# Unit 1 weighed in two pairs, and the prior laid out on 64 partitions

## The chip, the cores and the metric

The kernel runs on one core of a Trainium2 chip. The metric is the device time of one execution in microseconds (us); a number of executions are timed and their median is given. Beside the timed ones there is one profiled execution, whose records make up the profile and the trace.

## The reference

For each of 4096 rows (32 x 128) there are four heads of 4096 logits and four prior values. Each head's logits go through a softmax, the prior's four values go through a softmax, and the result is the mixture of the four heads by the prior.

```python
batch, seq, vocab = 32, 128, 4096
num_heads = 4
...
prior_probs = np.exp(prior - prior.max(axis=-1, keepdims=True))
prior_probs = prior_probs / prior_probs.sum(axis=-1, keepdims=True)
softmax = np.exp(logits - logits.max(axis=-1, keepdims=True))
softmax = softmax / softmax.sum(axis=-1, keepdims=True)
mixture = np.sum(prior_probs[..., None] * softmax, axis=2)
```

All is float32: 268 MB of logits are read, 67 MB of output are written, and the prior is 64 KB. The kernel takes the exp of the logits without subtracting their maximum.

## The kernel before

The 4096 rows are 32 units of 128 rows, one row on each partition. A unit has 8 MB of logits (four heads of 128 x 4096) and 2 MB of output. One Python loop over the units writes out the instructions; the order on each engine is the order written, apart from a few moves made at the end. Waits are given by hand: `only(ins, *keep)` leaves an instruction nothing to wait for but what it is given and what stands before it on its engine.

**Loads.** `load(u)` (line 111) issues the logits of unit u on ACT's DMA queue into `ltile[:, u % 2]`, so there are two slots. Units 0 and 28 to 30 are loaded in two halves, unit 31 in three parts, all others in one transfer of 8 MB. Loads 0 and 1 are issued at the start and wait for nothing. Load u of the later units waits for the first product of unit u - 2, which is the last to read that slot:

```python
if u >= 2:
    only(ld, adds[u - 2, 0] if h == 0 else exps[u - 2, to - 1])
```

While `late` holds, load u + 1 is written in the loop of unit u and then moved by `ahead` to stand on ACT just before the first exp of unit u. It is ACT that issues it, so what stands behind it on ACT comes after it, and it comes after what stands before.

**Exps.** For each head, ACT takes the exp of 128 x 4096 logits and sums the rows into `dsum` (line 176). Head 0 is done in place in `ltile`, heads 1 to 3 go to `ebuf1`, `ebuf2` (in PSUM) and `ebuf3`. The exp of head 1 waits for the second sum of the unit before, that of head 2 for its last sum, and in the middle units that of head 3 waits for the store of unit u - 2 (`free`).

**Weighing.** `weigh(h, n)` takes the reciprocal of n row sums on DVE (line 185), behind the last of their exps, and multiplies by the prior's n columns on GpSimd (POOL, line 187), which gives `coeff`. `sets` says which heads are weighed at once: all four in units 0 to 27, in pairs and single ones in the last four.

**Product and sums.** DVE multiplies head 0 by its coefficient into `obuf` (line 194, `adds[u, 0]`) and then adds heads 1 to 3 one after the other (line 200, `adds[u, 1]` to `adds[u, 3]`).

**Stores.** Unit u - 1 is stored (line 124) from SP's DMA queue, behind its last sum. The last units are stored from ACT's queue.

**Prior.** At the start SP issues the prior's load (line 149), 32 partitions of 128 rows with four values each. `early_transfers` moves it, and ACT's first load, ahead of the opening barrier. DVE subtracts the maximum (lines 151 and 152), ACT takes the exp (line 153, on ACT behind the three loads and ahead of the exps of unit 0), DVE sums, takes the reciprocal and multiplies (lines 154 to 156) and transposes 32 x 32 blocks into `pp` in four instructions (line 162). `pp[p, j, h, 2 g + 1]` is then the prior of row p, unit 2 g + j, head h. The first to read it is the coefficient of unit 0.

Of the kernel before, what the change touches and what calls it, by code (L numbers as in the profile page):

```python
# [7 lines left out]
FP32 = mybir.dt.float32  # L8
# [39 lines left out]
def kernel(  # L48
# [6 lines left out]
    nc = tc.nc  # L55
# [3 lines left out]
    B, S, H, V = logits.shape  # L59
    assert prior.shape == (B, S, H)  # L60
    assert out.shape == (B, S, V)
    P = 128
    J = 2
    R = P * J
    G = B * S // R
    U = G * J
# [1 line left out]

    lg = logits.rearrange("b s h v -> (b s) h v").rearrange("(g p j) h v -> g j p h v", p=P, j=J)
    ov = out.rearrange("b s v -> (b s) v").rearrange("(g p j) v -> g j p v", p=P, j=J)  # L70
    pv = prior.rearrange("b s h -> (b s) h").rearrange("(k r) h -> k r h", r=P)

    cpool = ctx.enter_context(tc.tile_pool(name="cpool", bufs=1))
    psum = ctx.enter_context(tc.tile_pool(name="psum", bufs=1, space=bass.MemoryType.PSUM))
# [5 lines left out]
    def only(ins, *keep):  # L80
        for k in keep:
            tc.add_manual_dep(
                ins.ins,
                k.ins.name,
                mybir.DependencyInfo(mybir.DependencyClass.Sync, mybir.DependencyReason.DATA),
                reason="all that this instruction waits for",
            )
        tc.declare_no_dep(
            ins.ins,
            group="loop",  # L90
            keep=[k.ins for k in keep] + before.get(ins.ins.engine, []),
            reason="covered by the waits that are kept",
        )
        tc.add_to_no_dep_group("loop", ins.ins)
        before[ins.ins.engine] = [ins.ins]
        return ins
# [2 lines left out]
    ltile = cpool.tile([P, 2, H, V], FP32, name="ltile")  # L99
    loads = {}  # L100
    exps = {}
    adds = {}
    stores = {}

    def load(u):
        if u == 0 or u >= U - 3:
            cuts = (0, 2, 3, 4) if u == U - 1 else (0, 2, 4)
        else:
            cuts = (0, H)
        for h, to in zip(cuts, cuts[1:]):  # L110
            ld = nc.scalar.dma_start(  # L111
                out=ltile[:, u % 2, h:to], in_=lg[u // J, u % J, :, h:to, :]
            )


            if u >= 2:
                only(ld, adds[u - 2, 0] if h == 0 else exps[u - 2, to - 1])
            else:
                only(ld)
            for k in range(h, to):  # L120
                loads[u, k] = ld

    def store(u, acc, eng, lo=0, hi=V):
        st = eng.dma_start(out=ov[u // J, u % J, :, lo:hi], in_=acc[:, lo:hi])
        stores[u] = only(st, adds[u, H - 1])

    assert 2 * G == 32
    pr = cpool.tile([2 * G, P, H], FP32, name="pr")  # L130
    pn = cpool.tile([2 * G, H, P], FP32, name="pn")
    pmax = cpool.tile([2 * G, P], FP32, name="pmax")
    pp = cpool.tile([P, J, H, 2 * G + 1], FP32, name="pp")


    dsum = cpool.tile([P, U, H], FP32, name="dsum")
# [9 lines left out]

    with tc.manual_schedule():
        load(0)
        nc.sync.dma_start(out=pr, in_=pv)
        load(1)  # L150
        nc.vector.reduce_max(pmax, pr, axis=AX.X)  # L151
        nc.vector.tensor_sub(pr, pr, pmax.unsqueeze(2).to_broadcast([2 * G, P, H]))  # L152
        nc.scalar.activation(pr, pr, AF.Exp)  # L153
        nc.vector.reduce_sum(pmax, pr, axis=AX.X)  # L154
        nc.vector.reciprocal(pmax, pmax)  # L155
        nc.vector.tensor_mul(  # L156
            pn.rearrange("k h r -> k r h"), pr, pmax.unsqueeze(2).to_broadcast([2 * G, P, H])
        )
        pq = pn.rearrange("k h (p j) -> k j h p", j=J)
        for t in range(P // 32):  # L160
            c = 1 - t // 2
            nc.vector.transpose(  # L162
                pp[32 * t : 32 * (t + 1), :, :, c : c + 2 * G],
                pq[:, :, :, 32 * (t % 2) : 32 * (t % 2 + 1)],
            )

        late = False
        for u in range(U):
            bufd = u < U - 2
            lt = ltile[:, u % 2]  # L170
            acc = obuf[:, u % 2] if bufd else lt[:, 0]
            es = (lt[:, 0], ebuf1, ebuf2, ebuf3) if bufd else [lt[:, h] for h in range(H)]
            ppu = pp[:, u % J, :, 2 * (u // J) + 1]

            def exp(h, *keep):
                ex = nc.scalar.activation(  # L176
                    es[h], lt[:, h], AF.Exp, accum_out=dsum[:, u, h : h + 1]
                )
                keep = (loads[u, h],) + keep
                if bufd and u and h in (1, 2):  # L180
                    keep += (adds[u - 1, 1 if h == 1 else H - 1],)
                exps[u, h] = only(ex, *keep)

            def weigh(h, n, *keep):
                rc = nc.vector.reciprocal(rden[:, u, h : h + n], dsum[:, u, h : h + n])  # L185
                only(rc, exps[u, h + n - 1])
                mul = nc.gpsimd.tensor_mul(  # L187
                    coeff[:, u, h : h + n], rden[:, u, h : h + n], ppu[:, h : h + n]
                )
                return only(mul, rc, *keep)  # L190

            def add(h, mul, lo=0, hi=V):
                if h == 0:
                    st = nc.vector.tensor_scalar(  # L194
                        out=acc[:, lo:hi], in0=es[h][:, lo:hi], scalar1=coeff[:, u, h : h + 1],
                        scalar2=None, op0=ALU.mult,
                    )
                    adds[u, h] = only(st, mul)
                else:
                    st = nc.vector.scalar_tensor_tensor(  # L200
                        out=acc[:, lo:hi], in0=es[h][:, lo:hi], scalar=coeff[:, u, h : h + 1],
                        in1=acc[:, lo:hi], op0=ALU.mult, op1=ALU.add,
                    )
                    adds[u, h] = only(st, mul, adds[u, h - 1])

            free = (stores[u - 2],) if bufd and u >= 2 else ()

            if u < U - 4:  # L210
                sets = ((0, H),)
            elif u == U - 2:
                sets = ((0, 2), (2, 3), (3, 4))
            else:
                sets = ((0, 2), (2, 4))
            for h in range(H):
                if h == 2 and 0 < u < U - 3:
                    store(u - 1, obuf[:, (u - 1) % 2], nc.sync)
                if h == 2 and u == U - 1:
                    store(u - 1, ltile[:, (u - 1) % 2, 0], nc.scalar)  # L220
                if h == 1 and late:
                    load(u + 1)
                    pairs.append((loads[u + 1, 0].ins, exps[u, 0].ins))
                    late = False
                exp(h, *(free if sets[0][1] == H and h == H - 1 else ()))
                g = next((g for g, to in sets if to == h + 1), None)
                if g is None:
                    continue
                mul = weigh(g, h + 1 - g, *(free if g == 0 and h < H - 1 else ()))
                for k in range(g, h + 1):  # L230
                    n = 2 if u == U - 1 and k == H - 1 else 1
                    w = V // n
                    for c in range(n):
                        add(k, mul, c * w, (c + 1) * w)
                        if n > 1:
                            store(u, acc, nc.scalar, c * w, (c + 1) * w)


            late = u + 2 < U - 3
            if u + 2 < U and not late:  # L240
                load(u + 2)

            if u == U - 2:
                for k in (u - 2, u - 1):
                    store(k, obuf[:, k % 2], nc.scalar)
# [30 lines left out]
```

The softmax here doesn't subtract the row's maximum and nothing guards it: scores larger than these inputs give would overflow.

## Time and profile before

| | us |
|---|---|
| median of 3 timed executions | 780.8 (780.71 to 780.85) |
| the profiled execution | 780.91 |
| its span, first to last record | 779.1 |
| exp of 128 x 4096 on ACT, mean | 3.60 |
| product on DVE (line 194), mean | 2.35 |
| one sum on DVE (line 200), mean | 4.48 |
| reciprocal 128x4, 128x2, 128x1 on DVE, mean | 0.178, 0.163, 0.157 |
| coefficient 128x4, 128x2 on POOL, mean | 0.203, 0.197 |
| issue to landing of an 8 MB load, median | 29.6 |
| issue to landing of the prior's 64 KB | 2.5 |

Times inside the profile are counted from the start of the span. A line of the timeline gives start, length, engine, source line, operation, output and input with shapes, how many instructions are merged, and in brackets the idle time of the engine just before and what ended it. "ACTq" and "SPq" are DMA issues on ACT and SP: their length is that of issuing, not of the transfer. A DMA share of 1.00 means that all 16 DMA engines of the core are moving data; in stretches of a few us the share can exceed 1, as a packet is put down to the stretch in which it is recorded.

### The profile page before, as it was taken

Reading aid. Unit: us, or ns where it says so; the run is one execution under the profiler, and the core shown is the slowest. Engines: PE = TensorE matmul, PEld = TensorE weight load, DVE = VectorE, ACT = ScalarE, POOL = GpSimd, SP = SyncE. Lnnn points to the kernel's source line nnn. Section 1 sums busy time; section 2 is a strip of 40 time slices with the busy share of each in tenths; the row PEclk is TensorE's granted clock in tenths of the full one; section 3 lists DMA queues with packets and bytes.
Section 4 is the critical chain, followed back from the end, with each engine's and each line's share of the span. In section 5 each row is a group of like instructions: output and inputs, shape, how many; then the busy total and the mean of one; then the engine's idle time right before and its main releaser. Section 6 shows DMA issues by size and latency. Waiting matters only on the chain.

```text
span 779.1 us, 620 instructions
## 1 busy us (share of the span) xinstructions
DVE 517.7 (66%) x175; ACT 472.2 (61%) x258; POOL 7.6 (1%) x41
## 2 busy tenths in 40 slices
DVE  2447865568655686556875558755577555788986
ACT  4376555765557755577555675556755567557782
POOL 0000000000000000000000000000000000000000
DMA  9999999999999999999999999999999999999998
GB/s 407 458 417 400 475 404 431 431 465 424 404 468 401 463 417 423 452 448 414 417 468 407 458 404 468 421 413 448 416 459 417 457 405 464 410 429 431 432 428 379
DMA packets 10131, 335.64 MB, mean 431 GB/s; under 512 B 1136, under 2 KB 1136, under 8 KB 1168
## 3 DMA queue, kind: packets, MB, share of 16 engines
q10 hardware_dynamic: 6048, 276.83, 82.2%
q1 hardware_dynamic: 4080, 58.79, 17.6%
q14 instruction: 3, 0.02, 0.0%
HBM read 268.50 MB, written 67.11 MB: 431 GB/s over the span
## 4 chain that ended last, share of the span: by engine, by line
DMA 60%; DVE 28%; ACT 9%; issue 2%; POOL 0%; DVEq 0%; ACTq 0%; POOLq 0%
DMA out_dram<-obuf 47%; DVE obuf L200 23%; DMA ltile<-in_logits_dram 13%; ACT ebuf L176 8%; DVE obuf L194 4%; DVE ltile L200 1%; ACT ltile L176 1%; POOL coeff L187 0%; DVE rden L185 0%; DVEq L271 0%; ACTq L111 0%; POOLq L271 0%; ACTq L176 0%
## 5 line engine op out<-in xcount | busy, mean ns | idle before, releaser
L200 DVE SCALAR_TENSOR_TENSOR obuf<-ebuf,coeff,obuf 128x4096 f32<-128x4096 f32 x90 | 403.6, 4484 | 3.8 <-POOL coeff L187 0.6
L176 ACT ACTIVATE ebuf<-ltile 128x4096 f32<-128x4096 f32 x90 | 324.1, 3601 | 33.3 <-DVE obuf L200 19.4
L176 ACT ACTIVATE ltile<-ltile 128x4096 f32<-128x4096 f32 x38 | 137.4, 3615 | 255.4 <-DMA ltile<-in_logits_dram 255.0
L185 DVE RECIPROCAL rden<-dsum 128x4 f32<-128x4 f32 (+2 forms) x37 | 6.4, 174 | 235.9 <-ACT ebuf L176 233.2
L194 DVE TENSOR_SCALAR obuf<-ltile,coeff 128x4096 f32<-128x4096 f32 x30 | 70.6, 2353 | 10.9 <-POOL coeff L187 10.9
L200 DVE SCALAR_TENSOR_TENSOR ltile<-ltile,coeff 128x4096 f32<-128x4096 f32 (+1 forms) x7 | 27.0, 3874 | 1.0 <-POOL coeff L187 0.9
L176 ACT ACTIVATION_READ_ACCUMULATOR ebuf<-ltile 128x1 f32 x90 | 16.8, 187 | 0.0
L187 POOL TENSOR_TENSOR coeff<-rden,pp 128x4 f32<-128x4 f32 (+2 forms) x37 | 7.4, 201 | 756.2 <-DVE rden L185 745.6
L176 ACT ACTIVATION_READ_ACCUMULATOR ltile<-ltile 128x1 f32 x38 | 7.1, 186 | 0.0
L194 DVE TENSOR_SCALAR ltile<-ltile,coeff 128x4096 f32<-128x4096 f32 x2 | 4.7, 2353 | 0.6 <-POOL coeff L187 0.6
L153 ACT ACT_TABLE_LOAD x1 | 1.3, 1283 | 2.2 <-issue 2.2
L151 DVE TENSOR_REDUCE pmax<-pr 32x128 f32<-32x512 f32 x1 | 0.7, 674 | 2.5 <-DMA pr<-in_prior_dram 2.5
L162 DVE STREAM_TRANSPOSE pp<-pn 32x256 f32<-32x256 f32 x4 | 1.7, 435 | 0.1
L154 DVE TENSOR_REDUCE pmax<-pr 32x128 f32<-32x512 f32 x1 | 0.7, 674 | 0.7 <-ACT pr L153 0.7
L156 DVE TENSOR_TENSOR pn<-pr,pmax 32x512 f32<-32x512 f32 x1 | 1.0, 1019 | 0.0
L155 DVE RECIPROCAL pmax<-pmax 32x128 f32<-32x128 f32 x1 | 0.9, 941 | 0.0
L153 ACT ACTIVATE pr<-pr 32x512 f32<-32x512 f32 x1 | 0.6, 628 | 0.5 <-DVE pr L152 0.5
L152 DVE TENSOR_TENSOR pr<-pr,pmax 32x512 f32<-32x512 f32 x1 | 0.7, 679 | 0.0
L260 POOL MEMSET const-bfloat16-1.0<- 128x1 bf16 x1 | 0.1, 102 | 0.0
L260 POOL MEMSET const-uint8-127<- 128x1 uint8 x1 | 0.1, 102 | 0.0
L260 POOL MEMSET const-float32-0.0<- 128x1 f32 x1 | 0.1, 99 | 0.2 <-issue 0.2
L260 POOL MEMSET const-float32-1.0<- 128x1 f32 x1 | 0.1, 99 | 0.0
## 6 DMA issues: line engine op xcount, KB each, us to landing
out_dram<-obuf SPq DMA_DIRECT2D x28, 2048.0 KB, 28.1
ltile<-in_logits_dram ACTq DMA_DIRECT2D x7, 4096.0 KB, 25.5
ltile<-in_logits_dram ACTq DMA_DIRECT2D x2, 2048.0 KB, 30.9
out_dram<-obuf ACTq DMA_DIRECT2D x2, 2048.0 KB, 26.6
out_dram<-ltile ACTq DMA_DIRECT2D x1, 2048.0 KB, 19.3
out_dram<-ltile ACTq DMA_DIRECT2D x2, 1024.0 KB, 4.8
ltile<-in_logits_dram ACTq DMA_DIRECT2D x28, 29.6
pr<-in_prior_dram SPq DMA_DIRECT2D x1, 64.0 KB, 2.5
```

Of the source, the lines that this page charges most:

```text
L151: nc.vector.reduce_max(pmax, pr, axis=AX.X)
L152: nc.vector.tensor_sub(pr, pr, pmax.unsqueeze(2).to_broadcast([2 * G, P, H]))
L153: nc.scalar.activation(pr, pr, AF.Exp)
L154: nc.vector.reduce_sum(pmax, pr, axis=AX.X)
L155: nc.vector.reciprocal(pmax, pmax)
L156: nc.vector.tensor_mul(pn.rearrange("k h r -> k r h"), pr, pmax.unsqueeze(2).to_broadcast([2 * G, P, H]))
L162: nc.vector.transpose(pp[32 * t : 32 * (t + 1), :, :, c : c + 2 * G], pq[:, :, :, 32 * (t % 2) : 32 * (t % 2 + 1)],)
L176: ex = nc.scalar.activation(es[h], lt[:, h], AF.Exp, accum_out=dsum[:, u, h : h + 1])
L185: rc = nc.vector.reciprocal(rden[:, u, h : h + n], dsum[:, u, h : h + n])
L187: mul = nc.gpsimd.tensor_mul(coeff[:, u, h : h + n], rden[:, u, h : h + n], ppu[:, h : h + n])
L194: st = nc.vector.tensor_scalar(out=acc[:, lo:hi], in0=es[h][:, lo:hi], scalar1=coeff[:, u, h : h + 1], scalar2=None, op0=ALU.mult,)
L200: st = nc.vector.scalar_tensor_tensor(out=acc[:, lo:hi], in0=es[h][:, lo:hi], scalar=coeff[:, u, h : h + 1], in1=acc[:, lo:hi], op0=ALU.mu ...
```

## The change

Two things change, and two follow from them.

1. The prior's 4096 rows lie on 64 partitions of 64 rows instead of 32 of 128. Partition q x 32 + k holds rows k x 128 + q x 64 onward. The source of its load thus has three dimensions, q, k and the 256 values of a partition. The arithmetic is the same with half the elements on each partition, and two transposes over 64 partitions take the place of four over 32.
2. Unit 1 is weighed in two pairs of heads. The first pair's coefficients are multiplied on DVE, the second pair's on POOL as before.
3. Load 3, which goes into unit 1's slot, waits for the reciprocal of unit 1's second pair, not for its first product. That reciprocal stands on DVE behind the product and the first sum of unit 1.
4. `recips` keeps the reciprocals by unit and head.

```diff
-    pv = prior.rearrange("b s h -> (b s) h").rearrange("(k r) h -> k r h", r=P)
+    pv = prior.rearrange("b s h -> (b s) h").rearrange("(k q r) h -> q k r h", q=2, r=64)
...
-            if u >= 2:
+            if u == 3:
+                only(ld, recips[1, 2])
+            elif u >= 2:
                 only(ld, adds[u - 2, 0] if h == 0 else exps[u - 2, to - 1])
...
-    assert 2 * G == 32
-    pr = cpool.tile([2 * G, P, H], FP32, name="pr")
-    pn = cpool.tile([2 * G, H, P], FP32, name="pn")
-    pmax = cpool.tile([2 * G, P], FP32, name="pmax")
-    pp = cpool.tile([P, J, H, 2 * G + 1], FP32, name="pp")
+    K = 2 * G
+    assert K == 32
+    pr = cpool.tile([2 * K, 64, H], FP32, name="pr")
+    pn = cpool.tile([2 * K, H, 64], FP32, name="pn")
+    pmax = cpool.tile([2 * K, 64], FP32, name="pmax")
+    pp = cpool.tile([P, J, H, K + 1], FP32, name="pp")
...
-        for t in range(P // 32):
-            c = 1 - t // 2
-            nc.vector.transpose(
-                pp[32 * t : 32 * (t + 1), :, :, c : c + 2 * G],
-                pq[:, :, :, 32 * (t % 2) : 32 * (t % 2 + 1)],
-            )
+        for a in range(2):
+            nc.vector.transpose(pp[64 * a : 64 * (a + 1), :, :, 1 - a : 1 - a + K], pq)
...
-                only(rc, exps[u, h + n - 1])
-                mul = nc.gpsimd.tensor_mul(
+                recips[u, h] = only(rc, exps[u, h + n - 1])
+                mul = (nc.vector if u == 1 and h == 0 else nc.gpsimd).tensor_mul(
                     coeff[:, u, h : h + n], rden[:, u, h : h + n], ppu[:, h : h + n]
                 )
...
-            if u < U - 4:
+            if u != 1 and u < U - 4:
                 sets = ((0, H),)
```

More of the change, by code (lines that the diff above doesn't have):

```diff
@@ L101 @@
     exps = {}
+    recips = {}
     adds = {}
@@ L151 @@
         nc.vector.reduce_max(pmax, pr, axis=AX.X)
-        nc.vector.tensor_sub(pr, pr, pmax.unsqueeze(2).to_broadcast([2 * G, P, H]))
+        nc.vector.tensor_sub(pr, pr, pmax.unsqueeze(2).to_broadcast([2 * K, 64, H]))
         nc.scalar.activation(pr, pr, AF.Exp)
@@ L156 @@
         nc.vector.tensor_mul(
-            pn.rearrange("k h r -> k r h"), pr, pmax.unsqueeze(2).to_broadcast([2 * G, P, H])
+            pn.rearrange("k h r -> k r h"), pr, pmax.unsqueeze(2).to_broadcast([2 * K, 64, H])
         )
         pq = pn.rearrange("k h (p j) -> k j h p", j=J)
-        for t in range(P // 32):
-            c = 1 - t // 2
-            nc.vector.transpose(
-                pp[32 * t : 32 * (t + 1), :, :, c : c + 2 * G],
-                pq[:, :, :, 32 * (t % 2) : 32 * (t % 2 + 1)],
-            )
+        for a in range(2):
+            nc.vector.transpose(pp[64 * a : 64 * (a + 1), :, :, 1 - a : 1 - a + K], pq)
         late = False
```

## The prediction

> **What bounds the kernel now.** I read the page's busy times and DMA rows first, then the timeline of the first 65 us, then the rates over one unit's period. The times of the vector and scalar engines say they are not the bound; the DMA rows say that the 16 DMA engines are.
>
> ```profile
> span 779.1 us, 620 instructions
> ...
> DVE 517.7 (66%) x175; ACT 472.2 (61%) x258; POOL 7.6 (1%) x41
> ...
> DMA  9999999999999999999999999999999999999998
> ...
> q10 hardware_dynamic: 6048, 276.83, 82.2%
> q1 hardware_dynamic: 4080, 58.79, 17.6%
> ...
> out_dram<-obuf SPq DMA_DIRECT2D x28, 2048.0 KB, 28.1
> ```
>
> The two queues fill 99.8% of the span: q10 carries what ACT issues, q1 what SP issues. Over any steady stretch of one unit (10.49 MB) the rate is flat:
>
> ```profile
> 77.66:101.84 24.18, 15.98 (x5) 14.65 (x9) 0.20 (x1) 1.00 1.00 434
> 101.84:126.02 24.18, 15.99 (x5) 14.69 (x9) 0.20 (x1) 1.00 1.00 434
> ```
>
> The columns are the stretch, its length, busy us of DVE, ACT and POOL, clock, DMA share, GB/s. So the kernel is a full DMA pipe with a lead-in of 1.3 us and a tail. It can gain nearly nothing; it loses whatever time the pipe runs dry. It can run dry only where a load is issued after the one ahead of it has landed, so I look at the start, where the changed code is:
>
> ```profile
> 0.00 0.39 SPq L149 DMA_DIRECT2D pr<-in_prior_dram  x1
> 0.12 2.03 ACTq L111 DMA_DIRECT2D ltile<-in_logits_dram  x3
> ...
> 2.50 0.67 DVE L151 TENSOR_REDUCE pmax<-pr 32x128 f32<-32x512 f32 x1 [2.50 <-DMA pr<-in_prior_dram]
> ...
> 3.92 0.63 ACT L153 ACTIVATE pr<-pr 32x512 f32<-32x512 f32 x1 [0.47 <-DVE pr L152]
> ...
> 12.25 3.62 ACT L176 ACTIVATE ltile<-ltile 128x4096 f32<-128x4096 f32 x1 [7.70 <-DMA ltile<-in_logits_dram]
> ...
> 29.30 0.18 DVE L185 RECIPROCAL rden<-dsum 128x4 f32<-128x4 f32 x1 [20.19 <-ACT ebuf L176]
> ...
> 32.18 0.33 ACTq L111 DMA_DIRECT2D ltile<-in_logits_dram  x1
> ...
> 41.31 3.62 ACT L176 ACTIVATE ltile<-ltile 128x4096 f32<-128x4096 f32 x1 [12.04 <-DMA ltile<-in_logits_dram]
> ...
> 58.73 0.33 ACTq L111 DMA_DIRECT2D ltile<-in_logits_dram  x1
> ...
> 64.51 3.62 ACT L176 ACTIVATE ltile<-ltile 128x4096 f32<-128x4096 f32 x1 [8.70 <-DMA ltile<-in_logits_dram]
> ```
>
> The prior lands at 2.50, its exp on ACT ends at 4.55 and ACT waits 7.70 us more for unit 0. Unit 0's first product ends at 32.18 and lets load 2 go, 9.1 us before load 1 is in (41.31). Load 3 goes at 58.73, 5.8 us before load 2 is in (64.51). Both are early enough.
>
> **The Trainium skill.** (1) "DMA: Bandwidth & Descriptors", Specifications, gives a fabric ceiling of 435 GB/s; the 434 above agrees, so a steady unit has nothing to give. (2) The same page, "Why a DMA increments its semaphore by 16 and not by 1", says how many engines a DMA uses: the largest number up to 16 that divides the slowest dimension not of size 1 on both sides, as the instruction carries it. Every DMA of before starts with 32 or 128 on both sides, so with 16; the trace agrees (q1 has 464 semaphore writes, 29 DMAs times 16), but shows no DMA with fewer. (3) The same page, "Queues, rings and completion order": each engine takes its queues in turn, a packet each. The trace agrees: on every engine a 64 KB load packet (2.418 us) and a 16 KB store packet (0.611 us) alternate, and even a 4 byte semaphore write takes a turn: the last store packets of unit 0 start by 70.18, its semaphore writes only at 72.83 to 73.20, one load packet later.
>
> **The change part by part.**
>
> Prior, the transfer. The built program of the changed kernel carries the source of the prior's load as 2 x 32 x 256 and the destination as 64 x 1 x 256; before, both were 32 x 512. By (2) it runs on 2 engines, not 16: 32 packets of 1 KB on each, where each engine had two of 2 KB. By (3) these take turns with the three loads that ACT issues at 0.12. In before the first prior packet starts at 1.02 and the first load packet at 1.29; in 0.27 us some 4 go ahead (a 2 KB packet had a median of 0.084 us, so I take 0.05 for 1 KB, an estimate). What remains is 28 and a semaphore write: 29 turns. Loads 0 and 1 hold 16 packets of 32 KB (1.213 us), 8 of 64 KB and 3 semaphore writes on each engine: 27 turns. So the prior lands with load 1: 41.3, plus 32 x 0.05 less the 0.17 of the two packets there before, 1.4, gives X = 42.7. Bounds: landing as now, 2.5, if (2) doesn't hold here; 38.8 if 8 packets get ahead; 43.8 at 0.084 each.
>
> Prior, the arithmetic. Half the elements per partition: DVE 0.67 + 0.68 and ACT 0.63 become about 0.41 each (0.15 fixed, as the smallest reciprocal's 0.155, and half of the rest), with gaps 1.35 us from landing to the end of the exp (bounds 1.0 to the 2.05 of now). Sums, reciprocal, product and two transposes (now 0.67 + 0.94 + 1.02 + 1.78) lie beside 14.5 us of ACT in unit 0 and cost nothing while they are under that.
>
> What queues behind. The prior's exp stands in ACT's queue ahead of unit 0's four exps; they can't start before X + 1.35 = 44.05, where now they start at 12.25. Four exps back to back take 14.5 (41.31 to 55.82 in unit 1), from their end to the issue of load 2 is 2.91 (55.82 to 58.73): load 2 is issued at 61.45. From issue to first packet was 1.17 for load 0 (0.12 to 1.29): 62.6. Now load 2 follows load 1 without a gap, whose last packets end at 40.4 to 40.9. So the pipe restarts 62.6 - 40.6 = 22.0 us late, with no store to fill it, since unit 0 has produced nothing.
>
> Unit 1. After that, T0 (unit 0's last sum) is 61.45 + 13.55 = 75.0; unit 1's third exp waits for it (75.0 to 78.7), the fourth ends at 82.4. On DVE: reciprocal, the coefficients there (128x2, not in the trace; taken as the reciprocal's 0.16 to 0.2), product 2.37 and one sum 4.50 from 75.0 end at 82.4, then the second reciprocal: load 3 goes at about 82.7, its first packet near 84. Load 2's packets end near 62.6 + 8 x 2.418 = 82, and store 0 (8 x 0.611 = 4.9 us on each engine, from about 80) covers to 86.9: no second gap. Waiting for the product as in before would have been 2.7 us later, 86.8, just covered too. In the schedule of before the edit would send load 3 at 56.3 rather than 58.73, behind a queue full to 64.5: nothing.
>
> From there the lateness is constant: unit 2's product ends near 102, load 3 near 108, the steady state has 5.5 us of such slack, and the exp, product and sums of one unit chain in 23.85 us against the pipe's 24.18. The tail is bound by bytes, as all that is left after 720 us goes through q10 in order. Sum: 780.91 (this execution; span 779.1) + 22.0 = 802.9; the median shown is 0.1 lower. I take 802.6.
>
> **The rivals.**
>
> No stall (the other side). The prior lands early enough: it spreads over 16 engines after all, or several packets go per turn. It decides at X + 1.35 + 14.5 + 2.91 + 1.17 = 40.6, that is X = 20.7: landed before that, load 2 still follows load 1. Then load 3's 2.4 us and store 1 some 6.5 us earlier change only the order in a full pipe; what can be won is the slow stretch at 46 to 50 and 60 to 62 us, where the DMA share stands 0.8 us above what the bytes need; what can be lost is some 0.2 us for 32 more packets. Time 780.8, 780.0 to 781.3. For it: the four packets ahead, and that no trace here shows a DMA on two engines. Against it: the alternation is strict wherever the trace shows two queues.
>
> Partial stall. Some turns take two packets, or more are ahead; X between 21 and 38.8, time 780.9 + (X - 20.7): at X = 33, 793. For it: the first packets of before overlap in the records, unlike the later ones.
>
> Late unit 1 alone: the prior does no harm, but store 1, issued earlier, takes two turns from load 3 (1.2 us) and the lateness grows. It counts in the tail only beyond the 2.35 us that DVE waits at 756.38, and needs two rounds of a load and a store packet (2.418 + 0.611 = 3.03 us): 780.8 + 6.06 - 2.35 = 784.5. Against it: exp 3 of unit 3 waits for store 1 till 100.14 now, and would start at 100.2.
>
> **How the numbers follow.** Full stall 0.73, 798.5 to 805; partial 0.10, half of it above 794; no stall 0.14; late unit 1 alone 0.02; faster by some effect at the start that I don't see 0.01. A measurement of this kernel tells about 0.2% (1.6 us) from no change: slower 0.85, same 0.14, faster 0.01. The range 794 to 805 leaves out 0.2.
>
> **What would show it.** Right: the prior's DMA takes about 42 us to land, not 2.5; the first unit's exp starts near 44 behind it; load 2 is issued near 61; the DMA row has a hole of about 20 us there and 9s after; 433 to 434 GB/s per unit later. Wrong: landing below 21 us with no hole (the no-stall rival), or between (partial); or further holes near 82 us, which would mean that load 3 came later than store 0 could cover.

## The result and the profile after

The changed kernel takes 803.48 us (median of 6 runs, 803.41 to 804.39) beside 780.78 for the kernel before on the same chip (6 runs, 780.66 to 780.97): a ratio of 1.0293, 95% interval 1.0279 to 1.0306. It is 22.7 us slower; 802.6 was forecast. The profiled execution took 803.69, its span is 801.9.

The page of the kernel after shows, in its 40 slices of 20 us, where the time is. The first row is ACT's busy tenths, the second the DMA engines', the third GB/s:

```profile
ACT  0076755567555577555577555576555676558782
...
DMA  9908999999999999999999999999999999999998
GB/s 402 437 1 366 419 467 396 458 445 401 450 416 447 451 418 426 458 405 458 407 435 453 445 418 448 401 446 451 412 458 403 434 458 423 440 418 440 423 429 382
```

One slice, 40 to 60 us, moves next to nothing, and the one behind it somewhat less than the rest (366 GB/s). ACT does next to nothing in the two slices ahead of the hole. The timeline of the kernel after says what ACT waited for:

```profile
0.00 0.68 SPq L155 DMA_DIRECT2D pr<-in_prior_dram  x1
0.12 2.20 ACTq L112 DMA_DIRECT2D ltile<-in_logits_dram  x3
...
43.03 0.41 DVE L157 TENSOR_REDUCE pmax<-pr 64x64 f32<-64x256 f32 x1 [43.03 <-DMA pr<-in_prior_dram]
...
43.92 0.42 ACT L159 ACTIVATE pr<-pr 64x256 f32<-64x256 f32 x1 [40.29 <-DVE pr L158]
44.24 3.60 ACT L178 ACTIVATE ltile<-ltile 128x4096 f32<-128x4096 f32 x1
...
58.76 0.18 DVE L187 RECIPROCAL rden<-dsum 128x4 f32<-128x4 f32 x1 [11.86 <-ACT ebuf L178]
...
61.64 0.33 ACTq L112 DMA_DIRECT2D ltile<-in_logits_dram  x1
...
82.74 0.33 ACTq L112 DMA_DIRECT2D ltile<-in_logits_dram  x1
...
85.77 3.62 ACT L178 ACTIVATE ltile<-ltile 128x4096 f32<-128x4096 f32 x1 [3.25 <-DMA ltile<-in_logits_dram]
```

The prior lands at 43.03 instead of 2.50. Unit 0's first exp (44.24) has no idle time of its own in front of it: it starts straight behind the prior's. Its logits have been there since about 12 us. Load 2 goes at 61.64, when load 1 has long been in, and that is the hole. The windows of the kernel after show it (stretch, length, busy us of DVE, ACT and POOL, clock, DMA share, GB/s):

```profile
0.00:40.50 40.50, 0.00 (x0) 1.28 (x1) 0.20 (x4) 1.00 0.98 415
40.50:62.50 22.00, 6.64 (x10) 15.29 (x10) 0.20 (x1) 1.00 0.00 1
62.50:84.00 21.50, 20.82 (x9) 14.25 (x8) 0.20 (x1) 1.00 1.00 402
...
125.50:149.68 24.18, 15.98 (x5) 14.73 (x9) 0.20 (x1) 1.00 1.00 434
```

From 40.5 to 62.5 us the pipe is all but empty. Before and behind it is full, and a later unit still moves at 434 GB/s in 24.18 us. The edges of that window were chosen; the trace's record of every DMA packet ("packet records" below; it names no engine, but a packet starts where the one ahead of it on its engine ends) measures the hole without them: between 39 and 70 us the 16 engines stand idle for 21.8 us on average, and in the kernel before not at all.

### The profile page after: what moved, and what is told of

It is laid out like the page before. It is cut to its first block, busy times and chain, and to the rows that moved or that the text cites. A ratio compares the mean times of both kernels' runs of the same rounds, so it can differ in the third digit from the quotient of the medians.

```text
span 801.9 us, 620 instructions
## 1 busy us (share of the span) xinstructions
DVE 515.3 (64%) x175; ACT 472.0 (59%) x258; POOL 7.6 (1%) x41
## 4 chain that ended last, share of the span: by engine, by line
DMA 59%; DVE 28%; ACT 9%; issue 2%; POOL 0%; DVEq 0%; ACTq 0%; POOLq 0%
DMA out_dram<-obuf 46%; DVE obuf L202 23%; ACT ebuf L178 9%; DMA ltile<-in_logits_dram 7%; DMA pr<-in_prior_dram 5%; DVE obuf L196 4%; DVE ltile L202 1%; ACT ltile L178 1%; POOL coeff L189 0%; DVE rden L187 0%; DVEq L274 0%; DVE pr L158 0%; DVE pmax L157 0%; ACT pr L159 0%; ACTq L112 0%
```

## The experiments

The theory is the prediction's: two engines because of the source's slowest dimension, turns with the loads, and ACT's order. Rivals: the packets' size or number, the weighing of unit 1, a transfer that is slow by itself.

**The prior in two transfers.** Everything as changed, but no dimension of 2:

```diff
-        nc.sync.dma_start(out=pr, in_=pv)
+        for q in range(2):
+            nc.sync.dma_start(out=pr[32 * q : 32 * (q + 1)], in_=pv[q])
```

> The changed kernel, but the prior comes in two transfers of 32 partitions each (q = 0, then q = 1), the rest as changed. Theory (the source's slowest dimension of 2 confines the transfer to 2 engines, whose packets take turns with the loads): each transfer now starts with 32 on both sides, uses 16 engines, lands by about 6 us, unit 0's first exp waits for load 0 again (about 12.2), no hole in the DMA row: 780.8 us, 780.2 to 781.2. Rival A (64 packets of 1 KB take turns with the loads however they are spread, or half-sized partitions are slow): still above 790. Rival B (the weighing of unit 1 costs a part of the 22.7 us): between 782 and 800.

Measured: 781.02 us (13 runs, 780.90 to 781.18), ratio 1.0003, interval 0.9995 to 1.0011. The timeline of this kernel:

```profile
0.00 1.25 SPq L156 DMA_DIRECT2D pr<-in_prior_dram  x2
...
8.81 0.41 DVE L158 TENSOR_REDUCE pmax<-pr 64x64 f32<-64x256 f32 x1 [8.81 <-DMA pr<-in_prior_dram]
...
12.37 3.62 ACT L179 ACTIVATE ltile<-ltile 128x4096 f32<-128x4096 f32 x1 [1.85 <-DMA ltile<-in_logits_dram]
```

The same 64 packets of 1 KB, the same partitions and the same weighing, and the whole loss is gone. The landing is still 6 us later than before (and 3 later than I had expected), but ACT still waits 1.85 us more for load 0, so it is hidden.

**The new prior alone, and the new weighing alone.** Each is one half of the change's diff laid on the kernel before. The kernel with the prior alone, as a difference from the changed kernel (the reciprocals are kept no longer, and all coefficients are on POOL again):

```diff
-            if u == 3:
-                only(ld, recips[1, 2])
-            elif u >= 2:
+            if u >= 2:
...
-            if u != 1 and u < U - 4:
+            if u < U - 4:
```

> Before with the new layout of the prior alone, unit 1 weighed as before. Theory: the prior lands at 43 again and the hole stays; load 3 goes 2.7 us later than in the changed kernel (85.4 against 82.7), which store 0 covers all or in part: 803.5 to 805. Rival B (the weighing costs something): below 803.

> Before with the weighing of unit 1 in two pairs and the earlier load 3 alone, the prior as before. Theory: load 3 goes at 56.3 instead of 58.7 into a queue that is full to 64.5, store 1 some 6.5 us earlier: 780.8, 780.2 to 781.2. Rival B: slower by more than 0.5 us. A gain of up to 0.8 us would mean that the slow stretches at 46 to 50 and 60 to 62 us go away.

Measured: the prior alone 804.99 us (4 runs, 804.05 to 805.60), ratio 1.0308 (1.0294 to 1.0322); the weighing alone 781.14 (13 runs, 780.88 to 781.34), ratio 1.0004 (0.9995 to 1.0012). So all of the loss comes with the prior, and the weighing neither costs nor gains what can be told. With the prior alone load 3 is issued at 85.17, with the weighing as well at 82.74: the gate on the second reciprocal sends it 2.4 us earlier behind the hole. Whether that gains anything there isn't settled by the times: the ratios differ by 0.0015 (1.2 us), but their intervals overlap. In the schedule of before it sends load 3 at 56.05 instead of 58.73, and unit 3, which it is for, starts no earlier: at 88.84, and at 88.11 in the kernel before. First the lines of the kernel with the weighing alone, then that of the kernel before.

```profile
56.05 0.34 ACTq L112 DMA_DIRECT2D ltile<-in_logits_dram  x1
...
88.84 3.62 ACT L179 ACTIVATE ltile<-ltile 128x4096 f32<-128x4096 f32 x1 [9.68 <-DMA ltile<-in_logits_dram]
```

```profile
88.11 3.62 ACT L176 ACTIVATE ltile<-ltile 128x4096 f32<-128x4096 f32 x1 [8.51 <-DMA ltile<-in_logits_dram]
```

**The same transfer without turns.** The 2 x 32 x 256 transfer, issued on ACT's queue ahead of load 0 (and load 0's first half still ahead of the barrier):

```diff
-        load(0)
-        nc.sync.dma_start(out=pr, in_=pv)
+        nc.scalar.dma_start(out=pr, in_=pv)
+        load(0)
```

> The changed kernel with the same transfer of the prior (2 x 32 x 256), but issued on ACT's queue ahead of load 0, so that its packets take no turns with the loads. Theory: 32 packets of 46 ns go through on 2 engines in about 1.5 us, the prior lands by about 4 us, no hole; the loads start some 0.7 us later and on two engines up to 2 us later: 781.5 to 783. Rival C (a transfer on 2 engines, or with three source dimensions, is slow by itself, whatever else is queued): it lands late again, and the loads behind it with it: above 800.

Measured: 784.74 us (4 runs, 782.77 to 785.13), ratio 1.0045 (1.0031 to 1.0059), 2 us above what I had expected. The landing in its timeline:

```profile
0.13 1.12 ACTq L154 DMA_DIRECT2D pr<-in_prior_dram  x1
1.29 1.63 ACTq L112 DMA_DIRECT2D ltile<-in_logits_dram  x3
...
3.51 0.41 DVE L157 TENSOR_REDUCE pmax<-pr 64x64 f32<-64x256 f32 x1 [3.51 <-DMA pr<-in_prior_dram]
...
15.77 3.62 ACT L178 ACTIVATE ltile<-ltile 128x4096 f32<-128x4096 f32 x1 [10.95 <-DMA ltile<-in_logits_dram]
```

The very transfer that took 43 us takes 3.4 when nothing stands between its packets, and by the packet records it still runs on two engines (two semaphore writes). So it isn't slow by itself; it is slow by its turns. The price is another: load 0's first half is in 3.5 us later. By the packet records its share on 14 engines ends about 1.4 us later than before, on the two that carried the prior another 2.4 us later, and those two are still 2.3 to 3.4 us behind at the last loads. I had counted that lag as a delay of the start; it is carried to the end.

**How many turns.** Only n of the 32 packets of each of the two engines come through a source with a slowest dimension of 2; the rest comes in a second, contiguous transfer over all 16 engines behind it (n is 16 or 8). The prior's rows are then permuted among the units, so the mixture is taken with other rows' priors.

```diff
-        nc.sync.dma_start(out=pr, in_=pv)
+        pc = prior.rearrange("b s h -> (b s) h").rearrange("(m r) h -> m r h", r=64)
+        nc.sync.dma_start(out=pr[: 2 * n], in_=pv[:, :n])
+        nc.sync.dma_start(out=pr[2 * n :], in_=pc[2 * n :])
```

> The changed kernel, but only 32 of the prior's 64 packets come by a source of 2 x 16 x 256 (16 on each of two engines), the other 32 by a second, contiguous transfer behind it; the prior's rows are permuted among the units. Theory (one packet or semaphore write per turn with a load packet): on the two engines 16 + 1 + 2 + 1 = 20 turns; by the changed kernel's records turn 20 stands at 29.6 us, so the prior lands at 30, 9 us past the point (21) from which it costs: 789.9 to 791. Rival (landing in proportion to the packets, half of 43): lands at 21.5, 780.8 to 782.

> The same with 16 packets by a source of 2 x 8 x 256 (8 on each of two engines) and the other 48 behind it, rows permuted likewise. Theory: 8 + 1 + 3 + 1 = 13 turns, turn 13 at 18.3 us, landing 18.7, which is below the point of 21: late, but hidden, 780.7 to 781.5. Rival (lateness costs in proportion, with no threshold): 22.7 x (18.7 - 2.5) / (43.0 - 2.5) = 9 us more, 790.

Measured with n = 16: 794.17 us (4 runs; three at 793.63 to 794.25, one at 803.92, which nothing here explains), ratio 1.020 (1.014 to 1.026). With n = 8: 783.92 (6 runs, 782.13 to 784.92), ratio 1.0035 (1.0022 to 1.0048). Both are above what I had expected. The landings, n = 16 first:

```profile
33.11 0.41 DVE L159 TENSOR_REDUCE pmax<-pr 64x64 f32<-64x256 f32 x1 [33.11 <-DMA pr<-in_prior_dram]
...
52.12 0.33 ACTq L112 DMA_DIRECT2D ltile<-in_logits_dram  x1
```

```profile
20.14 0.41 DVE L159 TENSOR_REDUCE pmax<-pr 64x64 f32<-64x256 f32 x1 [20.14 <-DMA pr<-in_prior_dram]
...
39.16 0.33 ACTq L112 DMA_DIRECT2D ltile<-in_logits_dram  x1
```

Each lands about one turn later than I had counted (one turn is 2.5 us beside 64 KB packets, 1.26 beside 32 KB): the first packet starts at 5.2 to 5.8, not at 4.4. From the landing to load 2 there are 19.0 us in both, as in the changed kernel (18.6). With n = 16 half the packets cost 13.3 us, where the rival of a landing in proportion had next to nothing. The prediction's own rule for a partial stall, 780.9 + (X - 20.7) for a landing at X, gives 793.3 for 33.11. With n = 8 the landing is 18 us late and next to no hole follows: the 9 us of the rival without a threshold don't appear. What appears is 3.1 us that I hadn't foreseen. Load 2 then comes just as the pipe runs out. By the packet records of the profiled execution, which is 3.6 us slower than before, 0.3 us are idle there; some 1.9 us, averaged over the engines, are in packets that take longer than in the kernel before, some of them even around 180 us; and the rest is mostly at the end, as three engines start load 2 about 1.8 us behind the others and never catch up. Why the packets take longer stays open.

**One contiguous transfer.** The same 64 packets of 1 KB in one transfer of 64 x 256 on both sides, rows permuted likewise:

```diff
-    pv = prior.rearrange("b s h -> (b s) h").rearrange("(k q r) h -> q k r h", q=2, r=64)
+    pv = prior.rearrange("b s h -> (b s) h").rearrange("(m r) h -> m r h", r=64)
```

> The changed kernel with the prior in one transfer of 64 contiguous partitions (64 x 256 on both sides): the same 64 packets of 1 KB in one transfer, but on 16 engines; the prior's rows are permuted among the units. Theory: 4 packets and a semaphore write on each engine, 5 turns at most: landing by 10 us, 780.8. Rival A (64 packets of 1 KB are the trouble): above 790.

Measured: 781.11 us (12 runs, 780.96 to 781.48), ratio 1.0003 (0.9995 to 1.0012); the prior lands at 10.21. With the first experiment this leaves the shape of the source as the cause, and not the size or the number of packets. Every slow source here has three dimensions as well as an outermost one of 2; none with three and a larger outermost one was run. That it is the 2 is argued from the number of engines, which was two each time.

**The prior's exp behind unit 0's.** The transfer stays as changed; the prior's exp and the DVE work after it are written behind the four exps of unit 0:

```diff
+        def prior_rest():
-        nc.scalar.activation(pr, pr, AF.Exp)
+            nc.scalar.activation(pr, pr, AF.Exp)
...
                 exp(h, *(free if sets[0][1] == H and h == H - 1 else ()))
+                if u == 0 and h == H - 1:
+                    prior_rest()
```

> The changed kernel with the prior's exp, and the prior's arithmetic on DVE after it, written behind the four exps of unit 0 instead of ahead of them; the transfer stays as changed. Theory (half of the hole is ACT's order: unit 0's exps, 14.5 us, stand behind the prior's): the prior still lands at 43, unit 0's exps run from 12.5 to 29.5 beside the loads, and from the landing to the issue of load 2 there are only 1.35 us to the end of the prior's exp, 2.6 on DVE, 0.5 for the coefficient and 2.4 for the product: load 2 at 49.8, first packets at 50.9, a hole of 10.3 us: 791 to 792.5. Rival (the time of the landing alone sets it, or the loads on the two engines): 803 again.

Measured: 791.62 us (4 runs, 791.49 to 792.55), ratio 1.0138 (1.0121 to 1.0155). The timeline of this kernel:

```profile
12.33 3.62 ACT L180 ACTIVATE ltile<-ltile 128x4096 f32<-128x4096 f32 x1 [8.74 <-DMA ltile<-in_logits_dram]
...
42.70 0.41 DVE L157 TENSOR_REDUCE pmax<-pr 64x64 f32<-64x256 f32 x1 [42.70 <-DMA pr<-in_prior_dram]
...
43.60 0.42 ACT L161 ACTIVATE pr<-pr 64x256 f32<-64x256 f32 x1 [13.66 <-DVE pr L158]
...
49.47 0.33 ACTq L112 DMA_DIRECT2D ltile<-in_logits_dram  x1
```

The landing is as late as in the changed kernel, yet 11.9 us of the 22.7 are gone: unit 0's exps now run beside the loads, where in the changed kernel they stood in line. By the packet records the hole is 9.6 us, for the 10.3 expected. The loss is thus made of two things, a late landing and an instruction of ACT that stood ahead of work it had nothing to do with.

None of these beats the kernel before; the nearest are within what the runs can tell.

## Why the prediction was right

**The bound.** A full pipe that loses the time it runs dry: right. The hole is 21.8 us by the packet records, the loss 22.7; that nothing else is lost is off by the 0.9 between them.

**Two engines.** Right, and shown from both sides: the packet records after have the prior on two engines (two semaphore writes), 32 packets each, and the two experiments that only spread them over 16 engines take the loss away. The pages' counts agree, before first:

```profile
DMA packets 10131, 335.64 MB, mean 431 GB/s; under 512 B 1136, under 2 KB 1136, under 8 KB 1168
```

```profile
DMA packets 10149, 335.64 MB, mean 419 GB/s; under 512 B 1122, under 2 KB 1186, under 8 KB 1186
```

After there are 64 packets between 512 B and 2 KB, the prior's, and 14 fewer tiny ones: 2 semaphore writes for 16.

**Turns.** Right: the records show the prior's packets 1.25 us apart while 32 KB packets run beside them and 2.5 us apart beside 64 KB ones. Off was the start. I had some 4 packets going ahead of the first load packet; none did. The first starts at 4.4 us, behind two load packets on each of the two engines. The issue itself took 0.68 us instead of 0.39, but that this is the reason isn't shown. It didn't matter for X, the landing: at 4 packets ahead or none, more are left than loads 0 and 1 have turns, and load 1's end frees the rest at once. So 43.0 for 42.7 is no credit to the count of the start. In the experiment with n = 16, where a turn more does matter, such a count was off by about 3 us.

**The chain from X.** The front part on DVE and ACT measured 0.41, 0.42 and 0.42 for the 0.41 each that I had put; load 2 was issued at 61.64 for 61.45; its first packets moved at 62.6 as forecast; load 3 at 82.74 for 82.7. (Unit 1's exp of head 1 started at 66.16, behind unit 0's first sum: it is the first that it waits for, not the second as the account of the kernel has it.) ACT's order as the second half of the cause was argued in the prediction and is shown by the last experiment.

**The rest of the sum.** I had 22.0 and no other term; the loss is 22.7. The rest is mostly in packets that took longer just behind the restart and again at the end of load 2: the window from 62.5 to 84.0 has 402 GB/s. By the packet records such lengthening between 40 and 90 us is 0.7 us, averaged over the engines, more than in before. With it, and with store 0's packets from 80.3 on, load 2 was through only at about 85, where the prediction had 82; the pipe stayed full. And 802.9 less 0.1 is 802.8: for the 0.2 that brought it to 802.6 the prediction gives no reason.

**Unit 1.** That the earlier load 3 gains nothing in the schedule of before was right. That waiting for the product as in before would be covered behind the hole as well is borne out by the trace of the kernel with the prior alone: by its packet records no engine runs dry between 70 and 120 us, though load 3 goes only at 85.17. The profiled execution is still 1.1 us longer than that of the changed kernel. Its hole is no longer (21.6 us); some 0.7 us are in packets that took longer, and most of the rest is at the end, where the engines finish further apart. Whether load 3's time has to do with either isn't shown.

**The rivals.** No stall and partial stall fell with the landing at 43.03. The point at which a later landing begins to open a hole, put at 20.7, fits 20.14 (0.3 us of hole) and 33.11 (a hole from about 41 to 53). That nothing is lost below it doesn't hold: the landing at 20.14 cost 3.1 us.

## What to carry to other kernels

Look at the order of the dimensions on both sides of a small transfer as well as at its bytes: a source with an outermost dimension of 2 had its 64 KB on two engines, and beside large transfers it landed at 43 us, not at 2.5. A small transfer that takes turns with large ones costs a large packet's time for each of its own packets on an engine, so give it few packets for each engine. Letting it go first in the same queue also takes the turns away, but here, on two engines, it still cost 3.9 us. And an instruction that waits for such a transfer doesn't belong ahead of work in an in-order engine that could do without it.

## What was not expected of the hardware

In these runs a DMA engine that fell behind in a full pipe stayed behind. With the prior on ACT's queue the two engines that carried it were 2.4 us late at load 1 and still 2.3 to 3.4 us late at the last loads, and with n = 8 three engines that started load 2 about 1.8 us late were about 2.2 us behind 700 us later. In the changed kernel the two engines were about 1.3 us late at load 1, and the hole wipes that out: all 16 start load 2 within 1 us.

In the kernels before and after, load packets that normally take 2.418 us took 0.1 to 0.9 us longer in a few rounds: just after a restart of the load queue (62.6 us after the change), just ahead of the first store packets (47.6 before, 77.7 after), and in load 2's last round (60.4 before, 81.1 after). Later load packets of these two kernels don't show it. With n = 8 and with the prior alone some do even around 180 us. No run here tells why.
